# Output projection of a memory attention: eight column tiles of 512 tokens replaced by Strassen's seven products with 256 tokens moving

## The chip, the cores and the metric

The kernel runs on one core of one Trainium2 chip. The metric is the device time of one launch in microseconds (us). Before the change the median of three runs is 795.74 us (794.84 to 796.38). The engines are named as in the profile: PE is TensorE, PEld its weight loads, DVE is VectorE, ACT is ScalarE, POOL is GpSimd and SP is SyncE, which issues most of the transfers.

## The reference, cut to what matters

One decoder layer works on 512 tokens of 1024 features in float32. A mixer is followed by a cross-attention of 4 heads (256 features each) into 256 memory tokens, and by a gated feed-forward layer:

```python
o = jnp.einsum("bhsm,bmhd->bshd", probs, v).reshape(bsz, s, D_MODEL)
return o @ w_o                                   # (512 x 1024) @ (1024 x 1024)
...
h = h + memory_cross_attention(rmsnorm(h, xattn_norm[l]), rmsnorm(mem, mem_norm[l]), w_q[l], w_kv[l], w_o[l])
h = h + swiglu(rmsnorm(h, ffn_norm[l]), w_gate_up[l], w_down[l])
```

The change is in `o @ w_o` and in the addition of its result to `h`.

## The kernel before, in words

**Precision.** A float32 product is made of three float32r matmuls: each operand is split into a rounded part ("hi", a cast on ACT) and the rest ("lo", a subtraction on DVE). `mm3` (L116 to L119) multiplies hi by hi, hi by lo and lo by hi into one PSUM accumulation. A weight unit is 128 x 1024 elements. It is loaded into a `raw` tile, cast to `whi` on ACT (L203), and its rest `wlo` is computed on DVE (L205).

**The order of the work.** `SPEC` is a list of strings, and each string is a slot. A token such as `o:3` or `U:0.1.0` names an item. In step t the kernel emits, in turns, what follows the matmuls of slot t-1 (`post`), what prepares slot t+1 (`prep`) and the loads and splits of the weights that slot t+1 needs (`advance`, L1342); then come the matmuls of slot t (`mm`). The framework orders each engine's instructions from this emission order and from what is ready, and adds the waits. There are six PSUM banks for `ps` tiles, and a double bank `pd`.

**The attention's end before.** `O:h` (`i_pv`, L1005) multiplies the probabilities of head h by its values: two PSUM banks, each 128 features x 512 tokens. Its `post` splits each bank into `t_oh` (ACT, L233) and `t_ol` (DVE, L241). Then `o:0` to `o:7` (`i_o`, L1025) each make 128 output features for all 512 tokens: 8 k-tiles x 3 matmuls, with a 128 x 128 piece of `w_o` stationary and 512 tokens moving. The `post` of `o:m` adds the bank to the residual stream `st["h1", m]` (DVE, L1033; features on the partitions, tokens along the free dimension), and scales the halves of 256 tokens by the gain of the next norm into `t_fa` and `t_fb` (ACT, L1039). After each second m it calls `forms("fg", i, ...)`, which prepares the stationary operands of the next layer. The items `H:r.c` (`i_turn`, L1198) transpose `h1` into token-major tiles.

**Strassen's products, as the next layers have them.** `product` (L1051) computes one of seven products of a 2 x 2 block multiplication in Winograd's form. `forms` (L1159) makes the seven token-side operands of one pair of k-tiles: 4 casts on ACT, and on DVE 4 additions or subtractions of 256 columns, 3 rests of 512 columns and one of 256. `load_strassen` (L148) and `split_unit` (L183) make the seven weight-side operands of a chunk. Quadrants are loaded through SP. Products 5 and 7 add a second quadrant by an accumulating transfer from the POOL queue (L172). Product 6 is an accumulating transfer from one SBUF tile into another (L211). Product 3 is an addition on DVE (L194). The products run in the order 1, 2, 5, 6, 3, 7, 4: 1, 6, 7 and 4 accumulate in bank pair A, 5 and 3 in B, 2 is C. After each product its bank is added to what it belongs to, so a product that continues in a bank waits until the bank was read. In these layers the tokens are stationary (128 x 128) and 512 columns of weights move.

In the item names of `SPEC`, `U:b.f.part` is product f of block b of the gate and up projection, `d` is the down projection, and `V:f` is product f of the values of the memory. Part 0 means the first chunk (pairs 0 and 1 of k-tiles), part 1 the second (pairs 2 and 3), parts 2 and 3 one pair each of the second.

Of the kernel before, what the change touches and what calls it, by code (L numbers as in the profile page):

```python
# [13 lines left out]
P = 128  # L14
# [14 lines left out]


CHUNKS = [("g", b, ks, 512) for b in range(5) for ks in ((0, 1), (2, 3))] + [("g", 5, (0, 1, 2, 3), 256)]
CHUNKS += [("v", 0, (0, 1), 512), ("v", 0, (2, 3), 512)]
CHUNKS += [("d", p, ks, 512) for p, ks in ((0, (0, 1)), (0, (2, 3)), (1, (4, 5)), (1, (6, 7)), (2, (8, 9)), (2, (10,)))]
XBC_ORDER = [8, 10, 0, 1, 2, 3, 9, 11, 4, 5, 6, 7]

# [26 lines left out]
def hybrid_block(ctx: ExitStack, tc: tile.TileContext, a: dict, out: bass.AP,  # L62
# [185 lines left out]
    add_unit("dt", a["w_dt"], KT * 96)  # L248
    idx = 0
    for name, cnt in (("xbc", 12), ("z", 8), ("v", 8), ("pw", 2), ("op", 8), ("os", 8),  # L250
                      ("k", 8), ("q", 8), ("o", 8)):
        for m in range(cnt):
            add_unit((name, m), wu[idx], 1024)
            idx += 1
# [750 lines left out]
    def i_pv(h):  # L1005
        it = Item()

        def mm():
            it.ps = []
            for d in range(2):  # L1010
                ps = PS("o")
                it.ps.append(ps)
                o = (h % 2) * 256 + d * P
                for mt in range(2):
                    vh, vl = st["V", mt, h // 2]
                    xh, xl = st["P", h, mt]
                    mm3(ps, vh[:, o:o + P], vl[:, o:o + P], xh, xl, mt == 0, mt == 1)

        def post():
            yield from splits([("o", 2 * h + d) for d in range(2)], [("o", 512)] * 2, it.ps)  # L1020

        it.mm, it.post = mm, post
        return it

    def i_o(m):  # L1025
        it = Item(keys=[("o", m)])

        def mm():
            proj(hold(it, "wo"), ready[("o", m)], [st["o", k] for k in range(8)])

        def post():
            h = st["h1", m]
            nc.vector.tensor_tensor(out=h, in0=h, in1=it.ps, op=ALU.add)  # L1033
            yield
            i, c = m // 2, m % 2
            if c == 0:
                st["F", i] = T("fa"), T("fb")
            for k in range(2):
                nc.scalar.activation(st["F", i][k][:, 256 * c:256 * c + 256], h[:, 256 * k:256 * k + 256],  # L1039
                                     AF.Identity, scale=col(V_FFN + m))  # L1040
            yield
            if c == 1:
                yield from forms("fg", i, *st["F", i])

        it.mm, it.post = mm, post
        return it


# [2 lines left out]
    def product(stage, block, f, part):  # L1051


        x = {"g": "fg", "d": "ff", "v": "mn"}[stage]
        tts = 1 if stage == "v" else 2
        chunks = [c for c, ch in enumerate(CHUNKS) if ch[0] == stage and ch[1] == block]
        pairs = [(c, i, n) for c in chunks for n, i in enumerate(CHUNKS[c][2])]
        width = CHUNKS[chunks[0]][3]
        begins, ends = part in (None, 0), part in (None, 1, 3)
        if part is not None:  # L1060
            one = chunks[min(part, 1)]
            pairs = [p for p in pairs if p[0] == one]
            if part >= 2:
                pairs = pairs[part - 2:part - 1]
            chunks = [one] if part < 3 else []
        it = Item(keys=[("s", c, f) for c in chunks])

        def mm():
            bank = (stage, BANK[f])
            if f in (1, 2, 5) and begins:  # L1070
                if bank == ("v", "A"):
                    st["vAB"] = psum.tile([P, 1024], F32, tag="pd", name=nm("vAB"), bufs=1)
                    st[bank] = [st["vAB"][:, 0:512]]
                elif bank == ("v", "B"):
                    st[bank] = [st["vAB"][:, 512:1024]]
                else:
                    st[bank] = [PS(stage + BANK[f]) for _ in range(tts)]
            it.ps = [t[:, :width] for t in st[bank]]
            for tt in range(tts):
                ts_ = slice(tt * P, (tt + 1) * P)  # L1080
                first = f in (1, 2, 5) and begins
                for c, i, n in pairs:
                    wh, wl = ready[("s", c, f)]
                    ws = slice(width * n, width * n + width)
                    xh, xl = st["X", x, f, i]
                    for p, w in ((xh, wh), (xl, wh), (xh, wl)):
                        nc.tensor.matmul(it.ps[tt], p[:, ts_], w[:, ws], start=first,  # L1087
                                         stop=(c, i, n) == pairs[-1] and p is xh and w is wl, skip_group_check=True)
                        first = False

        it.mm = mm
        return it, ends, width
# [221 lines left out]
    def num(t):  # L1314
# [8 lines left out]
        "o": i_o, "U": i_gu, "Y": i_turnff, "H": i_turn, "d": i_down, "G": i_gain,  # L1323
    }
    for line in (spec or SPEC):
        its = []
# [87 lines left out]
def _pack(inp):  # L1414
# [25 lines left out]
    u += [mtile(g["w_o"], m) for m in range(8)]  # L1440
    w_u = np.stack([f(t) for t in u])
    wd = g["w_down"].reshape(JF // 2, 2, P, 2, 512)
    wg = g["w_gate_up"].reshape(KT // 2, 2, P, 2, FF)
    wv2 = wkv[:, 1024:].reshape(KT // 2, 2, P, 2, 512)
    w_s = np.zeros((len(CHUNKS), 4, P, 1024), z32)
    for c, (stage, b, pairs, n) in enumerate(CHUNKS):
        for q, (r, k) in enumerate(((0, 0), (0, 1), (1, 0), (1, 1))):
            for j, i in enumerate(pairs):
                src = {"d": lambda: wd[i, k, :, r], "v": lambda: wv2[i, k, :, r],
                       "g": lambda: wg[i, k, :, r, 512 * b:512 * b + n]}[stage]  # L1450
                w_s[c, q, :, n * j:n * j + n] = src()
    dtp = np.zeros((KT, P, 96), z32)
# [43 lines left out]
```

## Time and profile before

| what | value |
|---|---|
| median of three runs | 795.74 us (794.84 to 796.38) |
| the profiled execution: device time, span | 796.13 us, 794.4 us |
| granted TensorE clock | 0.996 |
| PE busy | 782.7 us (99%), 3844 matmuls |
| PEld, DVE, ACT busy | 659.0, 632.9, 496.5 us |
| matmuls of the output projection (`wo`) | 192, starts from 411.2 to 456.0 us |

The span runs from the first to the last instruction of the profiled execution; 1.73 us of its device time lie outside. Stretches such as 411 to 456.4 are microseconds from the start of the span. A duration in the trace is that of one instruction from start to end; neighbouring instructions on an engine overlap, so what an instruction costs in a full queue is read from start to start.

### The profile page before, as it was taken

To read this page: it belongs to the slowest core of one execution; us is meant where nothing else is said; L and a number is where in the kernel's file an instruction comes from. 1 tells how busy PE (TensorE), PEld (TensorE's weight loads), DVE (VectorE), ACT (ScalarE), POOL (GpSimd) and SP (SyncE) were. 2 spreads that over 40 slices of the span, in tenths; PEclk is the share of its full clock that TensorE was granted. 3 is DMA by queue.
4 is the path that set the end of the run, shared out by engine and by line. 5 is a ranking of instruction groups with operands and counts; after the bars stand their busy time and mean duration, and the time that the engine had idled before them with its cause. 6 is when DMAs were issued, how large, how long until landed. Compare 5 with 4: busy or idle time off the path is not lost.

```text
span 794.4 us, 10540 instructions
## 1 busy us (share of the span) xinstructions
PE 782.7 (99%) x3844; PEld 659.0 (83%) x3844; DVE 632.9 (80%) x937; ACT 496.5 (63%) x791; POOL 49.8 (6%) x66
## 2 busy tenths in 40 slices
PE   9999999999999999999999999999999999999995
PEld 7878888888888889888888888888888888888984
DVE  7999969999895799675766667888866788867897
ACT  8668699657953547455655695665455665455845
POOL 0000000000000000000000011011101011101000
PEclk9999999999999999999999999999999999999998
DMA  8253335124475235765355268797779797869602
GB/s 331 90 172 106 114 92 179 54 100 132 153 261 162 97 106 149 170 176 171 132 131 142 72 135 228 176 263 148 247 159 282 179 245 164 248 156 269 163 14 106
DMA packets 41283, 128.62 MB, mean 162 GB/s; under 512 B 4864, under 2 KB 7296, under 8 KB 41232
## 3 DMA queue, kind: packets, MB, share of 16 engines
q1 hardware_dynamic: 33024, 99.30, 36.8%
q0 software_dynamic: 8064, 28.58, 19.8%
q8 instruction: 30, 0.49, 0.2%
q14 instruction: 21, 0.17, 0.1%
q10 hardware_dynamic: 144, 0.07, 0.0%
HBM read 116.63 MB, written 2.13 MB: 149 GB/s over the span
## 4 chain that ended last, share of the span: by engine, by line
PE 86%; DVE 8%; ACT 2%; DMA 1%; issue 1%; SPq 0%; DVEq 0%
PE gA L1087 15%; PE gB L1087 8%; PE dA L1087 5%; PE gC L1087 4%; PE dB L1087 2%; PE vAB L1087 2%; DVE wlo L205 2%; PE wo L117 2%; PE wo L119 2%; PE op L119 2%; PE op L117 2%; PE op L118 2%; PE q L117 2%; PE os L117 2%; PE q L118 2%; PE os L119 2%
## 5 line engine op out<-in xcount | busy, mean ns | idle before, releaser
L203 ACT CAST whi<-raw 128x1024 fp32r<-128x1024 f32 (+1 forms) x125 | 129.0, 1040 | 96.0 <-issue 14.2
L205 DVE TENSOR_TENSOR wlo<-raw,whi 128x1024 fp32r<-128x1024 f32 (+1 forms) x125 | 149.9, 1208 | 32.0 <-ACT whi L203 30.9
L203 ACT CAST whi<-wq 128x1024 fp32r<-128x1024 f32 (+1 forms) x76 | 77.4, 1028 | 76.2 <-PE gA L1087 19.3
L205 DVE TENSOR_TENSOR wlo<-wq,whi 128x1024 fp32r<-128x1024 f32 (+1 forms) x76 | 90.2, 1193 | 39.8 <-ACT whi L203 39.6
L172 POOL DMA_DIRECT2D raw<-w_s x38 | 32.7, 863 | 644.4 <-DVE t_vx L868 311.5
L1087 PE MATMUL gA<-whi,t_xh 128*128 128x512 f32 (+1 forms) x192 | 71.7, 373 | 0.0
L1087 PE MATMUL gA<-wlo,t_xh 128*128 128x512 f32 (+1 forms) x192 | 71.4, 372 | 0.0
L1087 PE MATMUL gA<-whi,t_xl 128*128 128x512 f32 (+1 forms) x192 | 71.3, 371 | 0.0
L1087 PEld LDWEIGHTS gA<-wlo,t_xh 128*128 128x128 f32 x192 | 36.2, 188 | 6.3
L1087 PEld LDWEIGHTS gA<-whi,t_xl 128*128 128x128 f32 x192 | 36.2, 188 | 6.2
L1087 PEld LDWEIGHTS gA<-whi,t_xh 128*128 128x128 f32 x192 | 36.2, 188 | 6.2
L1103 ACT ACTIVATE t_gu<-t_gu,s 128x512 f32<-128x512 f32 (+1 forms) x24 | 16.4, 688 | 31.7 <-DVE t_gu L1099 31.7
L1087 PE MATMUL dA<-whi,t_xh 128*128 128x512 f32 x88 | 34.1, 392 | 0.4 <-DVE t_hT L1244 0.2
L1087 PE MATMUL dA<-whi,t_xl 128*128 128x512 f32 x88 | 34.2, 389 | 0.0
L1087 PE MATMUL dA<-wlo,t_xh 128*128 128x512 f32 x88 | 34.1, 390 | 0.0
L194 DVE TENSOR_TENSOR wq<-wq,wq 128x1024 f32<-128x1024 f32 (+1 forms) x19 | 22.5, 1193 | 13.5 <-DMA wq<-raw 13.4
L1087 PE MATMUL gB<-whi,t_xq 128*128 128x512 f32 (+1 forms) x96 | 27.5, 371 | 0.0
L117 PE MATMUL z<-t_uh,whi 128*128 128x512 f32 x64 | 25.2, 394 | 0.4 <-ACT t_uh L233 0.4
L1165 ACT CAST t_xh<-t_x 128x512 fp32r<-128x512 f32 x30 | 18.6, 621 | 10.5 <-DVE t_x L1184 6.4
L117 PE MATMUL wo<-t_oh,whi 128*128 128x512 f32 x64 | 25.2, 394 | 0.0
L117 PE MATMUL v<-t_uh,whi 128*128 128x512 f32 x64 | 25.1, 392 | 0.0
L117 PE MATMUL q<-t_hgh,whi 128*128 128x512 f32 x64 | 25.1, 392 | 0.0
(401 smaller groups left out, 2242.5 us busy)
## 6 DMA issues: line engine op xcount, KB each, us to landing
raw<-w_u SPq DMA_DIRECT2D x68, 512.0 KB, 3.4
raw<-w_s SPq DMA_DIRECT2D x54, 512.0 KB, 4.4
wq<-w_s SPq DMA_DIRECT2D x36, 512.0 KB, 5.4
raw<-w_s POOLq DMA_DIRECT2D x36, 512.0 KB, 7.3
wq<-raw POOLq DMA_DIRECT2D x17, 512.0 KB, 7.8
t_x<-xT SPq DMA_DIRECT2D x16, 256.0 KB, 5.6
t_abc<-d_acs SPq DMA_DIRECT2D x16, 256.0 KB, 4.4
out<-t_hT SPq DMA_DIRECT2D x8, 256.0 KB, 2.3
```

Source lines behind the costliest of these rows:

```text
L117: nc.tensor.matmul(ps, whi, xhi, start=start, stop=False)
L118: nc.tensor.matmul(ps, whi, xlo, start=False, stop=False)
L119: nc.tensor.matmul(ps, wlo, xhi, start=False, stop=stop)
L172: nc.gpsimd.dma_start(sw[c, f][:, :n], quad("11" if f == 7 else "22"), accum_op=ALU.add)
L194: add = nc.vector.tensor_tensor(out=sw[c, 3][:, :n], in0=sw[c, 3][:, :n], in1=sw[c, 6][:, :n], op=ALU.add)
L203: nc.scalar.copy(hi[:, :n], raw[:, :n])
L205: nc.vector.tensor_tensor(out=lo[:, :n], in0=raw[:, :n], in1=hi.bitcast(F32)[:, :n], op=ALU.subtract)
L1087: nc.tensor.matmul(it.ps[tt], p[:, ts_], w[:, ws], start=first, stop=(c, i, n) == pairs[-1] and p is xh and w is wl, skip_group_check=True)
L1103: st["silu"] = nc.scalar.activation(g, g, AF.Silu, scale=st["r3",][:, c:c + 1])
L1165: nc.scalar.copy(h if w is None else h[:, w], src)
```

## The change

The eight items `o:0` to `o:7` become the seven products of a Strassen multiplication, named `W:f` in the order list. `w_o` moves from the weight units to two chunks of quadrants. The post of `O:h` now copies its two banks into `t_fa` and `t_fb` (ACT) and calls `forms("ao", h, ...)`. A product of this stage runs through the new `turned`: a 128 x 128 piece of the weights is stationary, and a half of 256 tokens moves, so that the result is feature-major as `h1` is. Four feature tiles share two banks. After each product four additions of 256 columns put it into `h1`. The gain scaling and `forms("fg", ...)` for pairs 0 and 1 follow product 3, those for pairs 2 and 3 product 4. The transposes `H:0.0` to `H:0.3` move behind product 4. The first block of the next layer takes its second chunk pair by pair.

```diff
-CHUNKS += [("v", 0, (0, 1), 512), ("v", 0, (2, 3), 512)]
+CHUNKS += [(x, 0, ks, 512) for x in "vo" for ks in ((0, 1), (2, 3))]
...
-    ... "O:3", "o:0", "o:1",
-    "o:2", "o:3", "o:4 H:0.0", "o:5 H:0.1", "o:6 H:0.2", "o:7 H:0.3",
-    "U:0.1.0 H:1.0 H:1.1", "U:0.2.0 H:1.2 H:1.3", "U:0.5.0", "U:0.1.1 U:0.2.1", "U:0.5.1", ...
+    ... "O:3", "W:1.0", "W:2.0", "W:5.0", "W:1.1 W:2.1", "W:5.1", "W:6", "W:3", "W:7", "W:4 H:0.0 H:0.1 H:0.2 H:0.3",
+    "U:0.1.0 H:1.0 H:1.1", "U:0.2.0 H:1.2 H:1.3", "U:0.5.0", "U:0.1.2 U:0.2.2", "U:0.1.3 U:0.2.3", "U:0.5.1", ...
...
@@ in i_pv, the item O:h
         def post():
-            yield from splits([("o", 2 * h + d) for d in range(2)], [("o", 512)] * 2, it.ps)
+            F = T("fa"), T("fb")
+            for k in range(2):
+                for d in range(2):
+                    nc.scalar.copy(F[k][:, 256 * d:256 * d + 256], it.ps[d][:, 256 * k:256 * k + 256])
+            yield
+            yield from forms("ao", h, *F)
...
+    def i_o(f, part=None):
+        it, ends, _ = product("o", 0, f, part)
+        def post():
+            r, k, sign = INTO[f]
+            for t in range(4):
+                h = st["h1", 4 * r + t][:, 256 * k:256 * k + 256]
+                nc.vector.tensor_tensor(out=h, in0=h, in1=it.ps[t // 2][:, 256 * (t % 2):256 * (t % 2) + 256],
+                                        op=ALU.add if sign > 0 else ALU.subtract)
+            yield
+            if f in (3, 4):
+                for i in (2 * r, 2 * r + 1):
+                    F = T("fa"), T("fb")
+                    for q in (1, 0):
+                        for c in range(2):
+                            m = 2 * i + c
+                            nc.scalar.activation(F[q][:, 256 * c:256 * c + 256],
+                                                 st["h1", m][:, 256 * q:256 * q + 256], AF.Identity,
+                                                 scale=col(V_FFN + m))
+                    yield
+                    yield from forms("fg", i, *F)
+        it.post = post if ends else None
+        return it
...
@@ in product, called where the stage is "o"
+        def turned():
+            for t in range(4):
+                o = slice(256 * (t % 2), 256 * (t % 2) + 256)
+                first = f in (1, 2, 5) and begins and t % 2 == 0
+                for c, i, n in pairs:
+                    wh, wl = ready[("s", c, f)]
+                    ws = slice(512 * n + P * t, 512 * n + P * t + P)
+                    xh, xl = st["X", x, f, i]
+                    for p, w in ((xh, wh), (xl, wh), (xh, wl)):
+                        nc.tensor.matmul(it.ps[t // 2][:, o], w[:, ws], p, start=first,
+                                         stop=(c, i, n) == pairs[-1] and p is xh and w is wl, skip_group_check=True)
+                        first = False
```

`INTO` (L1231, which the down projection uses too) says for each product into which half r of the output features and which half k of the tokens it is added, and with which sign: 1 and 2 into (0, 0), 6 and 3 into (0, 1), 5 and 7 into (1, 1), 4 into (1, 0).

More of the change, by code (lines that the diff above doesn't have):

```diff
@@ L250, in hybrid_block @@
     for name, cnt in (("xbc", 12), ("z", 8), ("v", 8), ("pw", 2), ("op", 8), ("os", 8),
-                      ("k", 8), ("q", 8), ("o", 8)):
+                      ("k", 8), ("q", 8)):
         for m in range(cnt):
@@ L1019, in post @@
         def post():
-            yield from splits([("o", 2 * h + d) for d in range(2)], [("o", 512)] * 2, it.ps)
+            F = T("fa"), T("fb")
[4 more added lines that the diff above has]
+            yield from forms("ao", h, *F)
         it.mm, it.post = mm, post
         return it
[L1025 to L1029, printed above, removed]
+    def i_o(f, part=None):
+        it, ends, _ = product("o", 0, f, part)
         def post():
-            h = st["h1", m]
-            nc.vector.tensor_tensor(out=h, in0=h, in1=it.ps, op=ALU.add)
-            yield
[L1035 to L1045, printed above, removed]
+            r, k, sign = INTO[f]
[3 more added lines that the diff above has]
+                                        op=ALU.add if sign > 0 else ALU.subtract)
+            yield
+            if f in (3, 4):
[10 more added lines that the diff above has]
+        it.post = post if ends else None
         return it
@@ L1051, in product @@
     def product(stage, block, f, part):
-        x = {"g": "fg", "d": "ff", "v": "mn"}[stage]
+        x = {"g": "fg", "d": "ff", "v": "mn", "o": "ao"}[stage]
         tts = 1 if stage == "v" else 2
@@ L1078, in mm @@
             it.ps = [t[:, :width] for t in st[bank]]
+            if stage == "o":
+                return turned()
             for tt in range(tts):
@@ L1322, in hybrid_block @@
         "r2": lambda: rm(rms2), "rt": i_r2t, "q": i_q, "S": i_score, "T": i_ptr, "V": i_v2, "vf": i_memforms, "O": i_pv,
-        "o": i_o, "U": i_gu, "Y": i_turnff, "H": i_turn, "d": i_down, "G": i_gain,
+        "W": i_o, "U": i_gu, "Y": i_turnff, "H": i_turn, "d": i_down, "G": i_gain,
     }
@@ L1439, in _pack @@
     u += [mtile(g["w_q"], m) for m in range(8)]
-    u += [mtile(g["w_o"], m) for m in range(8)]
     w_u = np.stack([f(t) for t in u])
@@ L1443, in _pack @@
     wg = g["w_gate_up"].reshape(KT // 2, 2, P, 2, FF)
+    wao = g["w_o"].reshape(KT // 2, 2, P, 2, 512)
     wv2 = wkv[:, 1024:].reshape(KT // 2, 2, P, 2, 512)
@@ L1449, in _pack @@
                 src = {"d": lambda: wd[i, k, :, r], "v": lambda: wv2[i, k, :, r],
+                       "o": lambda: wao[i, k, :, r],
                        "g": lambda: wg[i, k, :, r, 512 * b:512 * b + n]}[stage]
```

4 rows, old and new, of the table SPEC are left out of this document.

## The prediction

> **What bounds the kernel now.** I read the page first (span, busy shares, the chain that ended last), then PE's list of waits (us in total, times, longest), then the stretches of time.
>
> ```profile
> span 794.4 us, 10540 instructions
> PE 782.7 (99%) x3844; PEld 659.0 (83%) x3844; DVE 632.9 (80%) x937; ACT 496.5 (63%) x791; POOL 49.8 (6%) x66
> PE 86%; DVE 8%; ACT 2%; DMA 1%; issue 1%; SPq 0%; DVEq 0%
> ```
>
> ```profile
> PE warm L384 <- DVE ones L100: 1.2, 1, 1.2
> PE s L117 <- ACT whi L130: 0.7, 1, 0.7
> PE yo L119 <- DVE t_prl L241: 0.4, 1, 0.4
> PE z L117 <- ACT t_uh L233: 0.4, 1, 0.4
> PE dA L1087 <- DVE t_hT L1244: 0.2, 1, 0.2
> ```
>
> PE is the bound. Its listed waits are 2.9 us in all, none of them around the projection. So what PE saves there is saved in full, and what it waits in addition is lost in full. The question is which engine has room. Columns of the next rows: the stretch and its length, then busy us (instructions) of PE, PEld, DVE, ACT and POOL, the clock, the DMA share, GB/s.
>
> ```profile
> 400.20:412.80 12.60, 12.60 (x61) 10.48 (x60) 9.88 (x21) 7.81 (x18) 1.70 (x2) 1.00 0.69 160
> 411.00:456.40 45.40, 45.40 (x208) 37.54 (x207) 26.11 (x41) 23.51 (x44) 2.55 (x3) 1.00 0.37 93
> 480.00:500.00 20.00, 20.00 (x90) 16.53 (x90) 14.84 (x16) 9.62 (x12) 3.42 (x4) 1.00 0.91 233
> ```
>
> In the projection (411 to 456.4) DVE is busy for 26.1 of 45.4 us: 19 us of room, all of which the change will claim.
>
> **PE's part.** Start and duration of single matmuls, and of one weight load:
>
> ```profile
> 411.22 0.39 PE L117 MATMUL wo<-t_oh,whi 128*128 128x512 f32 x1
> ...
> 438.20 0.39 PE L119 MATMUL wo<-t_oh,wlo 128*128 128x512 f32 x1
> ```
>
> ```profile
> 397.23 0.28 PE L117 MATMUL sc<-t_kTh,t_qh 128*128 128x256 f32 x1
> ...
> 399.27 0.28 PE L119 MATMUL sc<-t_kTh,t_ql 128*128 128x256 f32 x1
> ```
>
> ```profile
> 397.35 0.19 PEld L119 LDWEIGHTS sc<-t_kTh,t_ql 128*128 128x128 f32 x1
> ```
>
> From 411.22 to 438.20 lie 119 steps of one 512-column matmul (five items of 24 matmuls): 0.2267 us each. In the scores 17 steps of one 256-column matmul, each with a load of its own, take 2.04 us: 0.120. The old stage has 8 x 8 x 3 = 192 matmuls: 43.5 us. The new one has 4 feature tiles x 4 pairs x 3 = 48 per product, 336 in all: 40.3 us. Strassen's 7/8 alone would give 38.1; two matmuls of 256 columns cost 0.240 where one of 512 costs 0.227, which takes 2.2 back. **PE saves 3.2 us.** The transposes of `h1` stay; they only move.
>
> [...]
>
> **DVE's part.** What an instruction costs in a full queue is read from start to start:
>
> ```profile
> 424.30 0.42 DVE L1174 TENSOR_TENSOR t_x<-t_fa,t_fb 128x256 f32<-128x256 f32 x1
> 424.64 0.42 DVE L1175 TENSOR_TENSOR t_x<-t_fb 128x256 f32<-128x256 f32 x1
> ...
> 426.58 1.46 DVE L1169 TENSOR_TENSOR t_xl<-t_x,t_xh 128x512 fp32r<-128x512 f32 x2
> 427.96 0.68 DVE L1033 TENSOR_TENSOR t_x<-t_x,wo 128x512 f32<-128x512 f32 x1
> 428.61 1.23 DVE L205 TENSOR_TENSOR wlo<-raw,whi 128x1024 fp32r<-128x1024 f32 x1
> ...
> 477.03 2.36 DVE L205 TENSOR_TENSOR wlo<-wq,whi 128x1024 fp32r<-128x1024 f32 x2 [1.67 <-ACT whi L203]
> ```
>
> ```profile
> L194 DVE TENSOR_TENSOR wq<-wq,wq 128x1024 f32<-128x1024 f32 x18 | 21.8, 1222 | 13.5 <-DMA wq<-raw 13.4
> ```
>
> ```profile
> L241 DVE TENSOR_TENSOR t_ol<-o,t_oh 128x512 fp32r<-128x512 f32 x8 | 5.4, 690 | 2.5 <-ACT t_oh L233 2.4
> ```
>
> One `forms` is 3.66 us (424.30 to 427.96). A weight rest is 1.14 (two last 2.36, one 1.22), and so is product 3's addition, of the same length. A 256-column addition is 0.34, a 512-column one from PSUM 0.65. The new additions are 256 columns from PSUM, which no row shows: between 0.34 and 0.65; I take 0.34, half of 0.65 being 0.33.
>
> Removed: 8 rests `t_ol` (5.4) and 8 additions into `h1` (5.2). Added: four `forms("ao")` (14.6), 14 weight rests for 8 (6.8), two additions for product 3 (2.3), 28 additions of 256 columns (9.5). Net 33.2 - 10.6 = **22.6 us more DVE work**, against 19 us of room.
>
> When is it wanted? I take the time from 400.2 (the scores of head 3 are done) to the start of `W:3`, before which nearly all of it is due. PE wants `W:3` after `O:3` and 192 matmuls: 411.2 + 192 x 0.120 = 434.2. By then DVE must have done:
>
> - what is left of the attention, with the first weight rest: 9.88 - 5.4 = 4.5 (the stretch 400.20:412.80 without `t_ol`);
> - four forms: 14.6;
> - nine further weight rests (products 1, 2, 5, 6, 3; two chunks each): 10.3;
> - two additions for product 3: 2.3;
> - the additions after products 1, 2 and 5, 12 x 0.34: 4.1.
>
> That is 35.8 us of work in 34.0 us. How densely DVE can run, where each form goes back and forth between ACT and DVE, is bounded by its densest stretch (160:180), its densest among the products (760:780) and the next one there (660:680):
>
> ```profile
> 160.00:180.00 20.00, 19.59 (x92) 16.09 (x91) 19.90 (x34) 11.32 (x18) 0.00 (x0) 1.00 0.36 118
> 660.00:680.00 20.00, 19.86 (x92) 16.18 (x92) 18.50 (x31) 10.95 (x16) 1.71 (x2) 1.00 0.67 154
> 760.00:780.00 20.00, 20.00 (x90) 16.34 (x89) 19.27 (x32) 12.21 (x23) 0.00 (x0) 1.00 0.08 14
> ```
>
> At 19.90 of 20 the work takes 36.0 us and is 2.0 late; two things can come off: 1.4 (the additions after product 2, whose bank nobody takes until the transposes) and 0.7 (the second chunk is first wanted 6 matmuls in). So the lower bound is no wait. At 18.50 it takes 38.7 and is 4.7 late. The nearest row, 19.27, gives 37.2 us, 3.2 late; I take off the 0.7, which is certain, and leave the additions where they are emitted, ahead of the later weights. **PE waits 2.5 us, bounds 0 and 4.7**; this wait is made of several, and comes once.
>
> Where it is seen first follows from the queue:
>
> ```profile
> 404.93 1.44 DVE L241 TENSOR_TENSOR t_ol<-o,t_oh 128x512 fp32r<-128x512 f32 x2
> 406.29 1.28 DVE L241 TENSOR_TENSOR t_Pl<-pT,t_Ph 128x512 fp32r<-128x512 f32 x2
> ```
>
> The rests `t_Pl` of head 3 stand behind the posts of `O:0` and `O:1`. What they emit grows from 2.9 us of `t_ol` to two forms (7.3). `O:3` wants its first `t_Pl` at about 408.7; if both forms run first, it is there at 404.9 + 7.3 + 0.6 = 412.8, 4.1 late, and if only head 0's does, at 409.2. PE has nothing else to run: `W:1.0` needs the banks that `t_Pl` still reads. Behind the waiting `O:3` stand its copies, head 3's forms, and for those `W:1.1`. It is the same DVE work seen earlier, so I don't add it.
>
> **ACT, transfers and banks** I cost at nothing.
>
> ```profile
> L203 ACT CAST whi<-raw 128x1024 fp32r<-128x1024 f32 x122 | 127.5, 1050 | 96.0 <-issue 14.2 <-PE wo L118 11.8 <-PE op L118 10.8
> L1165 ACT CAST t_xh<-t_x 128x512 fp32r<-128x512 f32 x30 | 18.6, 621 | 10.5 <-DVE t_x L1184 6.4 <-DVE t_x L1175 4.0
> L1165 ACT CAST t_xq<-t_fb 128x256 fp32r<-128x256 f32 x15 | 6.0, 402 | 0.0
> wq<-raw POOLq DMA_DIRECT2D x17, 512.0 KB, 7.8
> ```
>
> ACT in the same 34 us: at most 7.8 of the attention's end, 10 casts of weights (10.5), 16 copies at the 256-column price (6.4), four forms of 3 x 0.62 + 0.40 (9.0): 33.7 with the `t_oh` casts still in it, some 29 without them. It is not first; were DVE faster, ACT would be next. The transfers grow from eight units of 0.5 MB to 14 from HBM and two between SBUF tiles: 8 MB in 40 us or 200 GB/s, and the next layer runs at 233 GB/s and a share of 0.91 without a wait of PE (480:500). The last one due is product 6's accumulation for the second chunk: issued after the second `W:2` split, a slot ahead of `W:2.1`, with 7.8 to landing, 1.05 and 1.22 for the split, 10.1 us in all; PE's work from there is `W:1.1`, `W:2.1`, `W:5.1` and 6 matmuls, 9.4. It is 0.7 late if no other wait comes first, and hidden behind the 2.5. Banks: a product that follows in the same bank (7, then 4) waits for additions, but the loop over feature tiles is the outer one, so the first bank is free for half a product, 2.9 us, before it is wanted.
>
> **The seam into the next layer** I also cost at nothing.
>
> ```profile
> 456.40 0.69 DVE L1033 TENSOR_TENSOR t_x<-t_x,wo 128x512 f32<-128x512 f32 x1 [3.29 <-PE wo L119]
> 459.67 0.69 DVE L1178 TENSOR_TENSOR t_xl<-t_fa,t_xh 128x512 fp32r<-128x512 f32 x1
> ```
>
> From the last addition to the end of the first rest of the last form it took 4.0 us (456.40 to 460.36). Now two pairs follow product 4: 4.0 + 3.7 = 7.7 us. PE has cover: transposes and the slots `U:0.1.0`, `U:0.2.0`, `U:0.5.0`, 36 x 0.227 = 8.2 us without the transposes. Pairs 0 and 1 have the time of `W:7` and `W:4`, 11.5 us, for 13.4 of DVE work (two forms 7.3, eight additions 2.7, three weight rests 3.4), of which 1.5 (the last form's later rests) can follow. If the cover fails, it costs up to 1.9.
>
> **Sum.** -3.2 + 2.5 = -0.7. The profiled execution took 796.13, so 795.4; it lies 0.39 above the median, so 795.0 against 795.74.
>
> **Rivals.** A measurement of this kernel can tell about 0.2% (1.6 us) from no change.
>
> *DVE keeps up.* The weight rests move into DVE's gaps before 400 and the additions after product 2 later; the wait is 0.5: 795.74 - 2.7 = 793.0. For it: 19.90 of 20 in 160:180. Against it: PE had other work there, here every product waits for forms.
>
> *DVE falls behind further.* The mechanism is the to and fro within each form (ACT idles 10.5 us behind `t_x`, the row of L1165). It decides from a density of 0.906 down: there the wait is 4.8 and the sum +1.6. At 0.89 DVE takes 40.2 us, ends at 440.4, 5.5 late after the 0.7: +2.3, 798.0. For it: the ring `O:3`, copies, forms, `W:1.1` leaves DVE with little choice. Against it: 18.50 and 19.27 where the products were fed the same way.
>
> *Weight loads bound the smaller matmuls.* At one load of 0.188 per matmul 336 take 63.2 us, not 40.3: +19.7, 815. The rows of the scores speak against it: loads of 0.19 start every 0.12. [...]
>
> **How the numbers follow.** Forecast 0.42, DVE keeps up 0.32, falls behind 0.24, loads 0.02. So faster 0.32, same 0.42, slower 0.26. The forecast's own range is 794.1 to 797.3 (the wait's bound 4.7). For 8 in 10 I go down to the full saving, 792.4, and up to 798.4, where the density is about 0.88.
>
> **What would show it.** PE: 336 matmuls in the stage, 0.120 apart where they run. DVE over nine tenths busy from 400 to 436. PE waits naming `t_Pl` before `O:3`, `t_xl` before `W:1.1`, or `wlo` before `W:6` and `W:3`, 2.5 us in all, and none at `U:0`. I am wrong in the term if the step isn't 0.120, in the bound if the waits name DMA or ACT, in the place if they are at `U:0`.

## The result and the profile after

The changed kernel took 810.37 us (median of 4 runs, 809.87 to 811.82), the kernel before beside it 795.66 (794.84 to 796.38): a ratio of 1.0187, 95% interval 1.0175 to 1.0199. It is slower by 14.7 us. I had forecast 795.0 and a range up to 798.4: the prediction was wrong. In a later session one launch of the kernel before and the profiled one of the spread kernel ran at a mean granted clock of 0.56 and took 1320 and 1311 us; the ratios leave them out, and that trace is not used.

The profiled execution of the changed kernel took 809.87 us, 13.7 more than that of before. From its page the span, the busy shares and the chain that ended last:

```profile
span 808.0 us, 10957 instructions
PE 785.5 (97%) x3988; PEld 665.7 (82%) x3988; DVE 655.4 (81%) x989; ACT 510.3 (63%) x821; POOL 55.1 (7%) x72
PE 81%; DVE 10%; ACT 5%; issue 2%; DMA 1%; DVEq 0%; ACTq 0%
```

The chain that was 86% PE now runs through DVE and ACT for 15% (10% before). PE's list of waits from 396 to 500 us (us in total, times, longest), where before had none:

```profile
PE o L116 <- ACT t_Ph L232: 3.7, 1, 3.7
PE gA L1095 <- ACT t_xh L1187: 3.1, 2, 2.1
PE hT L1227 <- ACT t_hT L1231: 2.5, 2, 2.0
PE oA L1109 <- ACT t_fb L1022: 0.6, 1, 0.6
PE gB L1095 <- ACT t_hT L1231: 0.6, 1, 0.6
PE gC L1095 <- ACT t_hT L1231: 0.4, 1, 0.4
PE gA L1095 <- DVE t_xl L1200: 0.3, 1, 0.3
```

All but one name ACT, and they lie in two places: at `O:3` (seam 1, into the projection) and at the transposes and `U:0` (seam 2, out of it). The stretches (columns as in the prediction: length, busy us of PE, PEld, DVE, ACT, POOL, then the granted clock, the DMA share and GB/s) show something more:

```profile
400.00:411.00 11.00, 7.40 (x37) 5.84 (x35) 10.51 (x26) 8.18 (x24) 1.74 (x2) 1.00 0.54 102
411.00:420.00 9.00, 8.29 (x32) 6.89 (x33) 6.92 (x16) 5.64 (x16) 0.00 (x0) 0.62 0.00 0
420.00:440.00 20.00, 20.00 (x169) 20.00 (x168) 15.39 (x26) 7.33 (x8) 0.86 (x1) 1.00 0.51 156
458.00:470.00 12.00, 9.47 (x51) 7.43 (x51) 9.30 (x16) 11.51 (x24) 1.71 (x2) 0.99 0.66 140
470.00:480.00 10.00, 7.04 (x23) 4.56 (x21) 8.39 (x18) 7.10 (x13) 0.86 (x1) 0.84 0.61 138
```

Behind each seam's waits the clock is below 1 (0.62 from 411 to 420, 0.84 from 470 to 480). On PE's own rows at seam 1 (start, duration, matmul, idle before):

```profile
411.13 0.73 PE L116 MATMUL o<-t_Ph,t_Vh 128*128 128x512 f32 x2 [3.73 <-ACT t_Ph L232]
412.44 0.58 PE L1109 MATMUL oA<-t_xh,whi 128*128 128x256 f32 x1 [0.57 <-ACT t_fb L1022]
...
413.46 0.63 PE L118 MATMUL o<-t_Ph,t_Vl 128*128 128x512 f32 x1
413.89 0.63 PE L116 MATMUL o<-t_Ph,t_Vh 128*128 128x512 f32 x1
...
418.58 0.28 PE L1109 MATMUL oA<-t_xh,wlo 128*128 128x256 f32 x1
418.70 0.29 PE L1109 MATMUL oA<-t_xh,whi 128*128 128x256 f32 x1
...
420.50 0.28 PE L1109 MATMUL oC<-t_xh,whi 128*128 128x256 f32 x1
...
458.43 0.29 PE L1109 MATMUL oA<-t_xh,wlo 128*128 128x256 f32 x1
```

After the wait, matmuls of 512 columns stand 0.43 apart instead of 0.227, at a granted clock of 0.50 (412.4 to 418.4), until 418.4, 7 us behind the wait. Then the projection runs without a wait: from 420.50 (`W:2.0`) to 458.43 lie 311 steps, 37.93 us with five transposes of 0.11 put among them, so 0.120 a step.

I divide the layer's middle by four marks, the same in every kernel with the products: the start of `O:0`, the first matmul into `oC` (`W:2.0`), the last into `oA` (`W:4`), and the first of `U:0.3`.

| kernel after, us | measured | without waits, from before's steps | lost |
|---|---|---|---|
| `O:0` to first `oC` | 22.38 | 14.7 (11.83 in before up to the projection, + 24 x 0.120) | 7.7 |
| first `oC` to last `W` | 37.93 | 37.9 | 0 |
| last `W` to `U:0.3` | 35.28 | 25.4 (24.52 in before, + 7 x 0.12 for 27 transposes instead of 20) | 9.9 |

At seam 1 waits of 4.30 (3.73 + 0.57) leave 3.4 of the 7.7 to the half clock; at seam 2 waits of 6.9 leave 3.0 of the 9.9 to the clock and smaller gaps. 7.7 + 9.9 less the 3.2 saved is 14.4; the three stretches measure 95.59 us against 81.11, 14.5 more. (`O:0` itself started 1.3 earlier; the span is 13.6 longer.)

What stands ahead of the late casts is read from ACT's queue. At seam 1:

```profile
406.50 0.64 ACT L1022 COPY t_fa<-o 128x256 f32<-128x256 f32 x2
...
409.97 0.62 ACT L1187 CAST t_xh<-t_x 128x512 fp32r<-128x512 f32 x1 [0.94 <-DVE t_x L1206]
410.50 1.07 ACT L232 CAST t_Ph<-pT 128x512 fp32r<-128x512 f32 x2
```

The transposes of head 3's weights (`T:3`) were done at 405, but the casts `t_Ph` stand behind the forms of head 0 and the copies and forms of head 1, and these in turn wait for DVE. At seam 2:

```profile
460.41 0.58 ACT L1231 COPY t_hT<-hT 128x512 f32<-128x512 f32 x1
461.02 0.64 ACT L1234 ACTIVATE t_sq<-t_hT 128x512 f32<-128x512 f32 x1
...
465.52 0.64 ACT L1234 ACTIVATE t_sq<-t_hT 128x512 f32<-128x512 f32 x1
466.06 0.18 ACT L1234 ACTIVATION_READ_ACCUMULATOR t_sq<-t_hT 128x1 f32 x1
466.15 0.89 ACT L1045 ACTIVATE t_fb<-t_x,vec 128x256 f32<-128x256 f32 x2
```

Four copies and squares of the transposed residual (`H:0.0` to `H:0.3`), 460.41 to 466.15, stand ahead of the scaling for pair 2. DVE had made this pair's last two additions some 6 us before (the first two of these three, 0.34 each):

```profile
458.96 1.07 DVE L1036 TENSOR_TENSOR t_x<-t_x,oA 128x256 f32<-128x256 f32 x3
...
461.16 0.41 DVE L1036 TENSOR_TENSOR t_x<-t_x,oA 128x256 f32<-128x256 f32 x1
```

PE waits for pair 2's cast until 469.35:

```profile
469.35 0.89 PE L1095 MATMUL gA<-whi,t_xh 128*128 128x512 f32 x2 [2.15 <-ACT t_xh L1187]
...
480.24 0.66 PE L1227 MATMUL hT<-ident,t_x 128*128 128x128 f32 x4 [1.95 <-ACT t_hT L1231]
```

The second row is what comes of it later: the copies of `H:1.0` and `H:1.1` stand behind pair 3's forms and hold the banks that the last transposes want.

### The profile page after: what moved, and what is told of

It is laid out like the page before. It is cut to its first block, busy times and chain, and to the rows that moved or that the text cites. A ratio compares the mean times of both kernels' runs of the same rounds, so it can differ in the third digit from the quotient of the medians.

```text
span 808.0 us, 10957 instructions
## 1 busy us (share of the span) xinstructions
PE 785.5 (97%) x3988; PEld 665.7 (82%) x3988; DVE 655.4 (81%) x989; ACT 510.3 (63%) x821; POOL 55.1 (7%) x72
## 3 DMA queue, kind: packets, MB, share of 16 engines
q0 software_dynamic: 8928, 31.72, 21.9%
## 4 chain that ended last, share of the span: by engine, by line
PE 81%; DVE 10%; ACT 5%; issue 2%; DMA 1%; DVEq 0%; ACTq 0%
PE gA L1095 14%; PE gB L1095 7%; PE dA L1095 5%; PE gC L1095 3%; DVE wlo L204 3%; PE dB L1095 2%; PE vAB L1095 2%; PE op L118 2%; PE op L116 2%; PE op L117 2%; PE q L116 2%; PE os L116 2%; PE q L117 2%; PE os L118 2%; PE q L118 2%; PE os L117 2%
## 5 line engine op out<-in xcount | busy, mean ns | idle before, releaser
L202 ACT CAST whi<-raw 128x1024 fp32r<-128x1024 f32 (+1 forms) x123 | 126.8, 1039 | 87.5 <-PE op L117 14.1
L204 DVE TENSOR_TENSOR wlo<-raw,whi 128x1024 fp32r<-128x1024 f32 (+1 forms) x123 | 147.3, 1208 | 33.6 <-ACT whi L202 32.6
L202 ACT CAST whi<-wq 128x1024 fp32r<-128x1024 f32 (+1 forms) x84 | 85.9, 1030 | 80.7 <-PE dA L1095 17.8
L204 DVE TENSOR_TENSOR wlo<-wq,whi 128x1024 fp32r<-128x1024 f32 (+1 forms) x84 | 100.0, 1196 | 41.2 <-ACT whi L202 40.9
L171 POOL DMA_DIRECT2D raw<-w_s x42 | 36.2, 868 | 636.9 <-DVE t_vx L867 310.3
L193 DVE TENSOR_TENSOR wq<-wq,wq 128x1024 f32<-128x1024 f32 (+1 forms) x21 | 24.9, 1196 | 15.6 <-DMA wq<-raw 15.6
L1187 ACT CAST t_xh<-t_x 128x512 fp32r<-128x512 f32 x38 | 23.6, 622 | 12.4 <-DVE t_x L1206 6.5
L1191 DVE TENSOR_TENSOR t_xl<-t_x,t_xh 128x512 fp32r<-128x512 f32 x38 | 25.2, 686 | 0.4
```

What stands on the lines that cost most here:

```text
L171: nc.gpsimd.dma_start(sw[c, f][:, :n], quad("11" if f == 7 else "22"), accum_op=ALU.add)
L193: add = nc.vector.tensor_tensor(out=sw[c, 3][:, :n], in0=sw[c, 3][:, :n], in1=sw[c, 6][:, :n], op=ALU.add)
L202: nc.scalar.copy(hi[:, :n], raw[:, :n])
L204: nc.vector.tensor_tensor(out=lo[:, :n], in0=raw[:, :n], in1=hi.bitcast(F32)[:, :n], op=ALU.subtract)
L1187: nc.scalar.copy(h if w is None else h[:, w], src)
L1191: nc.vector.tensor_tensor(out=dst, in0=src, in1=h.bitcast(F32), op=ALU.subtract)
```

## The experiments

My theory after this reading: the projection itself does what was forecast; the loss is the order of ACT's queue at two seams, and the clock behind each wait. The rivals: the waits only move when the order is changed, because the sum of ACT's or DVE's work is too large; or the smaller matmuls cost time that no wait shows.

**Seam 1 alone.** Head 1's forms become an item of their own behind `T:3`:

```diff
+            if h == 1:
+                st["F", h] = F
+            else:
+                yield from forms("ao", h, *F)
...
-    "V:4 S:3 O:0", "O:1", "T:3 O:2", "O:3"
+    "V:4 S:3 O:0", "O:1", "T:3 f:1 O:2", "O:3"
```

> The changed kernel, with head 1's forms emitted after the split of head 3's probabilities (t_Ph, t_Pl) in place of ahead of it. Theory A (queue order): the 3.7 us for which O:3 waits on t_Ph, and the 5.4 us at half clock behind it, come from two heads' forms standing ahead of that split on ACT and DVE; with one of them moved the wait is 1 us or less, the clock stays at 1.0 in the ten us that follow, and the time falls by 6 to 7.5 us, to 803 to 804.5. Theory B (my ledger: DVE has more work than time until W:3, in whatever order): the wait moves to W:1.0, W:1.1 or W:3 and at most 2 us are gained, 808.4 or more.

Measured: 807.01 us, ratio 1.0136 (1.0119 to 1.0153), 3.4 us less than the changed kernel. PE's waits at this seam:

```profile
PE oA L1115 <- ACT t_fb L1022: 1.4, 1, 1.4
PE o L116 <- ACT t_Ph L232: 0.8, 1, 0.8
```

They fell from 4.3 to 2.2 us (0.8 of them for `t_Ph`), the clock from 411 to 420 is 1.00, and `O:0` to `oC` takes 17.51 instead of 22.38. Of the 4.9 us gained here, 1.6 was lost at seam 2 (36.89 for 35.28). So theory A holds for the wait and the clock; the time lies between the two theories' ranges. (The profiled launch itself took 809.49: it began `O:0` 2.4 us later than the changed kernel's, 1.7 of them from a wait at 55 us, which this edit does not touch.)

**The clock at seam 1.** Sixteen matmuls whose result nothing reads fill the wait ahead of `O:3`:

```diff
+            if h == 3:
+                for _ in range(16):
+                    nc.tensor.matmul(fill[:, 0:512], vh[:, 0:P], vh, start=True, stop=True)
```

> The changed kernel, with 16 matmuls of 512 columns between O:2 and O:3 whose result nobody reads (3.6 us of PE work, just the length of the wait). No data comes earlier. If the half clock after the wait follows from PE having been idle, the matmuls after O:3 starts are 0.227 us apart in place of 0.43, and some 2.9 us are gained: 807 to 808. If they are slow because of what else runs then (ACT and DVE at the same operands), nothing is gained: 810.

Measured: 810.63 us, 1.0177 (1.0157 to 1.0197), no gain. In place it did what was expected: clock 1.00 from 411 to 420, and `O:0` to `oC` 19.59, 2.8 less. But seam 2 took 37.68, 2.4 more, with waits of 6.2 us in all (6.9 in the changed kernel) and a lower clock (0.76 and 0.83 from 470 to 490, for 0.84 and 1.00):

```profile
411.00:420.00 9.00, 8.32 (x54) 7.01 (x53) 8.35 (x18) 7.76 (x19) 0.00 (x0) 1.00 0.00 0
470.00:480.00 10.00, 7.47 (x24) 5.03 (x22) 7.51 (x13) 7.79 (x15) 0.86 (x1) 0.76 0.52 118
480.00:490.00 10.00, 9.30 (x35) 7.38 (x36) 4.66 (x11) 8.04 (x18) 0.00 (x0) 0.83 0.17 54
```

So how much clock a seam loses is not fixed by its waits alone. It differs from launch to launch too: of this kernel's four, one took 807.92 us at a mean clock of 0.995, and two took 811.2 at 0.990 and 0.991. A gain at one seam can only be trusted once the other is free of waits.

**Seam 2: transposes earlier on PE.**

```diff
-    "W:7", "W:4 H:0.0 H:0.1 H:0.2 H:0.3",
+    "W:7 H:0.0 H:0.1 H:0.2 H:0.3", "W:4",
```

> The changed kernel, with the transposes H:0.0 to H:0.3 in the slot of W:7 in place of that of W:4, so that their copies and squares on ACT (four of about 1.2 us) are done before product 4 ends. Theory A (ACT's queue at the second seam): the scaling for pairs 2 and 3 starts at once after the additions, some 4.8 us earlier; PE's waits at the start of the next layer (6.9 us) fall to 2 or less; 803 to 805.5. Theory B (DVE has fallen behind there): the waits stay, less than 1.5 us gained.

Measured: 812.38 us, 1.0206 (1.019 to 1.0221), 2.0 us above the changed kernel, with intervals that just overlap; the waits at seam 2 stayed (7.1 us). On ACT nothing was won: the copies and squares kept their place ahead of the scaling,

```profile
461.20 0.58 ACT L1231 COPY t_hT<-hT 128x512 f32<-128x512 f32 x1
...
466.94 0.89 ACT L1045 ACTIVATE t_fb<-t_x,vec 128x256 f32<-128x256 f32 x2
```

and PE lost the transposes as cover behind `W:4`. What matters is the place in ACT's queue, not when PE is done with the transposes.

**Both of these.** Seam 1's forms late and the transposes early:

> Both order changes (head 1's forms after the split of head 3's probabilities; transposes with product 7). If the two seams are independent and are the whole loss, the gains add: 796 to 798, still short of the 792.5 that PE's matmuls alone would give, with what is left in small waits. If DVE's ledger is the limit, a wait of 2 to 4 us on t_xl or wlo appears inside the W products, which the late start hid until now: 799 to 802.

Measured: 810.09 us, 1.0172 (1.0149 to 1.0194), above both ranges: the gains did not add, and no wait for `t_xl` or `wlo` stands inside the `W` products. Seam 1 kept most of its gain (19.04 to `oC`, with a clock of 0.81 from 411 to 420), seam 2 took 37.83 with a clock of 0.68 from 470 to 480.

**Seam 2: transposes later.** Two transposed blocks share the double bank, and the first is emitted behind `U:0.2.0`, so that ACT scales and forms pairs 2 and 3 first:

```diff
-    "W:7", "W:4 H:0.0 H:0.1 H:0.2 H:0.3",
-    "U:0.1.0 H:1.0 H:1.1", "U:0.2.0 H:1.2 H:1.3", "U:0.5.0", "U:0.1.2 U:0.2.2", "U:0.1.3 U:0.2.3", "U:0.5.1",
+    "W:7", "W:4", "U:0.1.0", "U:0.2.0 H:0.0", "U:0.5.0 H:0.1", "U:0.1.2 U:0.2.2 H:1.0", "U:0.1.3 U:0.2.3 H:1.1", "U:0.5.1",
```

> The changed kernel with the eight transposes into the next layer (`H:`) done two at a time in the double bank, and the first of them only behind `U:0.2.0`, so that on ScalarE the copies and squares of the transposed residual stand behind the scaling and the forms of pairs 2 and 3 instead of ahead of them. Theory A (the second half of the loss is ScalarE's queue: four copies and squares, some 4.9 us, ahead of the scaling that waits only for `W:4`): the first wait of the stage for a cast of pair 2 goes from 2.15 us to under 0.5, the waits behind `W:4` from 6.9 us to under 2, the half clock there goes too, and the stretch from the last `W` matmul to `U:0.3` falls from 35.3 us to 26 to 29; time 801 to 804. Rival B (ScalarE simply has too much work there, and the order only decides who is late): the waits move to the copies (the double bank, or the gate's `r3`) and come to some 6 us again; time 808 to 811. Rival C (the loss given back elsewhere, as with the earlier filler): in this stretch the gain shows, the total does not move.

Measured: 804.56 us, 1.0107 (1.0092 to 1.0122), 5.8 us less than the changed kernel. Seam 2:

```profile
PE hT L1228 <- ACT t_hT L1235: 2.9, 3, 1.2
PE gA L1094 <- ACT t_gu L1130: 0.6, 1, 0.6
PE gB L1094 <- DVE t_xl L1190: 0.2, 1, 0.2
```

The casts of pair 2 are in time. Of 6.9 us of waits 3.7 are left, now mostly at the double bank (2.9), whose copies stand close together on ACT; last `W` to `U:0.3` is 29.96, and the clock there is 1.00. Theory A holds for the casts, but its sizes don't: waits of 3.7 for under 2, 29.96 for 26 to 29, and a time 0.6 above its range. Rival B has a part in it, the waits for the bank.

**Both seams, and `T:3` earlier.** The last kernel with head 1's forms late as well, and then with one more line:

> The kernel of the late transposes with the forms of head 1 behind the post of `T:3` as well: both seams mended, the products themselves as in the changed kernel. Theory A (the whole loss of 14.7 us lies in the two seams, waits and the half clock behind them, and the products save 3 us): O:0 to the first `oC` 17.5 us, last `W` to `U:0.3` 26 to 29, time 796 to 800, that is within 0.5 per cent of the kernel before. Rival D (the matmuls with 256 columns, or the additional work of VectorE, cost time that is not seen as a wait in the two seams): time 803 or more with both seams free of waits.

Measured: 802.30 us, 1.0076 (1.0061 to 1.0091); `O:0` to `oC` 18.93, last `W` to `U:0.3` 29.97. Neither theory's time: both seams still wait (2.2 and 3.7 us). Seam 1 has the same two waits as with its repair alone (0.8 and 1.4), where it took 17.51 at a clock of 1.00; here the clock from 411 to 420 is 0.84, and with the transposes early it was 0.81.

```diff
-    "V:4 S:3 O:0", "O:1", "T:3 f:1 O:2", "O:3",
+    "S:3 V:4 O:0", "T:3 O:1", "f:1 O:2", "O:3",
```

> As the kernel with both seams mended, and the transposes of head 3's weights (`T:3`) one place earlier, ahead of `O:1`, with `S:3` ahead of `V:4`, so that the casts of these weights stand ahead of the copies of heads 1 and 2 on ScalarE. If what is left at the first seam (0.8 us for a cast of `t_Ph`, 1.4 us for a copy that frees a bank) comes from that order: no wait named t_Ph before `O:3`, O:0 to the first `oC` 15 to 16.5 us (the new place of `T:3` adds its 1.1 us to this stretch), 1 to 2 us less than with both seams mended. If it comes from the sum of ScalarE's work: the wait moves to the banks of `W:1.0`, and the time is the same within 0.5 us.

Measured: 801.81 us, 1.0076 (1.006 to 1.0093). No wait names `t_Ph`, as expected, and `O:0` to `oC` fell to 16.91, just above the range, since PE now waited 1.1 for `t_p`. The time fell by only 0.5, but not for the reason that the second outcome gives, a wait at the banks of `W:1.0`: what was won here was lost at seam 2. Seam 2, where nothing was changed and the waits were 2.9 for the bank as before, took 31.72 instead of 29.97, with the clock at 0.73 (470 to 480) for 1.00. Its rows:

```profile
472.18 1.09 PE L1234 MATMUL hT<-ident,t_x 128*128 128x128 f32 x8 [0.60 <-ACT t_hT L1241]
474.44 1.79 PE L1234 MATMUL hT<-ident,t_x 128*128 128x128 f32 x8 [1.16 <-ACT t_hT L1241]
477.39 1.97 PE L1234 MATMUL hT<-ident,t_x 128*128 128x128 f32 x8 [1.16 <-ACT t_hT L1241]
...
479.68 0.63 PE L1100 MATMUL gA<-whi,t_xl 128*128 128x512 f32 x1
480.11 0.63 PE L1100 MATMUL gA<-wlo,t_xh 128*128 128x512 f32 x1
```

The second eight transposes already take 1.79 us where the first took 1.09, so the clock had fallen after waits of 0.60 and 1.16.

**Moving the transposes in the kernel before.** One part of the change alone, with no Strassen product in the projection:

```diff
-    "o:4 H:0.0", "o:5 H:0.1", "o:6 H:0.2", "o:7 H:0.3",
+    "o:4", "o:5", "o:6", "o:7 H:0.0 H:0.1 H:0.2 H:0.3",
```

> The kernel before, its projection unchanged, with nothing but the four transposes `H:0.0` to `H:0.3` moved from behind `o:4` to `o:7` to behind `o:7`, all four, as the changed kernel has them behind `W:4`. On ScalarE four copies and squares then stand in the midst of the scaling of the last pair. Theory A (the place of the transposes makes a part of the loss by itself): the casts of pair 3 come 3.5 to 5 us later, TensorE waits before `U:0.1.1` or `U:0.2.1` 1 to 4 us, with a clock below 1 behind it; time 797 to 801. Rival E (only with all scaling behind the last product is there a loss; here pairs 0 to 2 are done early and cover it): no wait over 0.5 us between `o:7` and `U:0.3`, time 795 to 796.5.

Measured: 800.07 us, 1.005 (1.0035 to 1.0065), 3.8 us slower than before. Theory A's time is right; its place is not. No cast of pair 3 kept PE waiting, but the bank of a later transpose and a bank of `U:0` did, and the clock fell to 0.83 from 470 to 480:

```profile
470.36 0.66 PE L1205 MATMUL hT<-ident,t_x 128*128 128x128 f32 x4 [1.61 <-ACT t_hT L1209]
471.59 0.79 PE L1087 MATMUL gB<-whi,t_xh 128*128 128x512 f32 x1 [0.57 <-ACT t_hT L1209]
```

So moving the transposes, which changes no arithmetic, and that I had costed at nothing ("they only move"), costs 3.8 us by itself in the kernel before.

**Spreading the transposes.** On top of the kernel with `T:3` earlier, the four pairs are spread, the copies of the second half go to DVE, and the first silus wait for the squares in an item of their own (`R`):

```diff
-                nc.scalar.copy(st["h", c, r], ...)
+                (nc.vector.tensor_copy if r else nc.scalar.copy)(st["h", c, r], ...)
...
-    "U:0.2.0 H:0.0", "U:0.5.0 H:0.1", "U:0.1.2 U:0.2.2 H:1.0", "U:0.1.3 U:0.2.3 H:1.1", "U:0.5.1", "U:0.6", "U:0.3",
+    "U:0.2.0", "U:0.5.0", "U:0.1.2 U:0.2.2", "U:0.1.3 U:0.2.3 H:0.0", "U:0.5.1", "U:0.6.0 H:0.1", "U:0.6.1 H:1.0", "U:0.3 H:1.1 R",
```

> On top of the kernel with both seams mended and `T:3` early: the four pairs of transposes are spread between `U:0.1.3`, the two halves of `U:0.6`, and `U:0.3`, with 2.7 us or more of matmuls between two of them; the copies of the second half of the tokens go from ScalarE to VectorE, which idled 4.7 us there; and the first two silus of block 0 wait for the squares in an item of their own. Theory A (what was left at the second seam, 2.9 us of waits for the double bank and some 3 us of half clock behind them, comes from the copies standing close together on ScalarE): no wait of hT over 0.3 us, clock 1.00 from 458 to 490, last `W` to `U:0.3` 27 to 28.5 us instead of 31.7 (with one pair more behind `U:0.3`), time 795 to 797, at most 1.5 us above what the sum of TensorE's work gives (792.5 plus the 2.2 us lost at the first seam). Rival B (ScalarE has too much work there whatever the order): the bank copies of `U:0.1` and `U:0.5` become late instead, 3 us or more of waits named t_gu, time 799 to 802.

Measured: 795.93 us, 1.0003 (0.9994 to 1.0012), 5.9 less than without it, in theory A's range; its signs at seam 2 are read in the trace of the next kernel, which has the same seam 2. Then with `T:3` behind `O:1` (`"S:3 V:4 O:0", "O:1 T:3", "f:1 O:2", "O:3"`):

> As the spread kernel, but `T:3` behind `O:1` instead of ahead of it, since ahead of it TensorE waited 1.1 us for the normalised weights of head 3. If the wait for t_p is only a matter of 2.7 us more cover: it goes, the casts of `t_Ph` come at about the same time (behind the copies of `O:1`), and O:0 to the first `oC` is 15 to 16.3 us against 16.9; time 0.5 to 1.5 us below the spread kernel, 794 to 796. If the wait moves to `O:3` (t_Ph or t_Pl late by the copies of `O:1`): the same time within 0.5 us.

Measured: 796.11 us, 1.0008 (0.9999 to 1.0017), no difference. The second outcome: the wait for `t_p` is gone, but one of 1.3 for `t_Ph` took its place, and `O:0` to `oC` is 16.91, as in the kernel with `T:3` ahead of `O:1`. Seam 2 in its trace has no wait in PE's list at all, the clock is 1.00, and last `W` to `U:0.3` takes 25.32 (with one pair of transposes behind it), less than the 27 to 28.5 expected:

```profile
470.00:480.00 10.00, 9.76 (x50) 7.91 (x51) 6.60 (x9) 9.63 (x21) 0.23 (x1) 1.00 0.80 211
```

ACT is still busy for 9.63 of 10 us here, so a full ACT need not hold PE up. But not only the order changed: with four copies on DVE, ACT is busy for 30.56 of the 37 us from 453 to 490, where the kernel with `T:3` earlier had 33.17 and the changed kernel 32.25. No run parts the order from these 2.6 us.

**Head 0's forms late too** (`if h < 2`, `"f:0 f:1 O:2"`):

> As the spread kernel with `T:3` behind `O:1`, and the forms of head 0, like those of head 1, only behind the casts of `t_Ph` and subtractions of `t_Pl` that `O:3` waits for (both heads' forms in turn, step by step). In that kernel TensorE still waited 1.3 us for `t_Ph`, since ScalarE made head 0's forms first. If only the order matters: no wait before `O:3` over 0.3 us, `W:1.0` starts without one, since it needs just the first cast and the first rest of heads 0 and 1; O:0 to the first `oC` 14.9 to 15.7 us against 16.9; time 793.8 to 795.0, that is 0.8 to 2 us below the kernel before, what is left of the 3.2 us that the products save. If ScalarE and VectorE together have too much work between `O:0` and `W:2.0`: the wait goes to `W:1.0` or `W:5.0` (t_xh, t_xl), 1 to 2 us, time 795.3 to 796.5, no difference from before.

Measured: 795.52 us against 795.91, 0.9995 (0.9986 to 1.0004): no difference that can be told. `O:0` to `oC` took 15.04 as expected; the wait went to `W:5.0` instead, 0.6 us of the 1 to 2 that the other outcome named, and for a copy that frees a bank (`t_fb`), not for `t_xh` or `t_xl`:

```profile
PE oB L1114 <- ACT t_fb L1021: 0.6, 1, 0.6
PE gB L1100 <- DVE t_xl L1208: 0.2, 1, 0.2
```

Its span is 793.4, 1.0 below that of before. PE stands idle there for 1.2 us between 400 and 480 (from the stretches), so 2.0 of the 3.2 should be left. Some 1 us I can't place, or 1.6 by the medians: this launch was 0.4 below its kernel's median, and the profiled one of before 0.4 above.

**What a wait costs.** The kernel before with a wait made on purpose: twelve copies on ACT ahead of head 3's casts, their result not read.

```diff
+            if h == 3:
+                for _ in range(12):
+                    nc.scalar.copy(T("sq"), it.ps[1])
```

> The kernel before with one artificial wait and nothing else: behind `T:3`, twelve copies of the transposed weights from PSUM to a scratch tile (about 0.53 us each, 6.4 us; the result is not read) stand on ScalarE ahead of the casts of head 3's `t_Ph`, so that TensorE waits before `O:3` some 4 us. Theory A (the clock falls after a wait of this length and costs as much again in part): the granted clock is 0.6 or so in the 5 to 7 us behind the wait, the projection's first matmuls stand 0.45 apart, and the time rises by the wait and 2 to 4 us more: 801.5 to 804. Rival F (the low clock behind the wait belongs to the new kernel's matmuls, not to the wait): clock 1.00 behind it, the time rises by the wait alone, 799 to 800.5.

Measured: 802.25 us, 1.0078 (1.0065 to 1.0091), 6.3 us more for a wait of 3.8:

```profile
411.38 1.22 PE L117 MATMUL o<-t_Ph,t_Vh 128*128 128x512 f32 x2 [3.79 <-ACT t_Ph L233]
...
413.25 0.63 PE L117 MATMUL o<-t_Ph,t_Vh 128*128 128x512 f32 x1
413.68 0.63 PE L118 MATMUL o<-t_Pl,t_Vh 128*128 128x512 f32 x1
...
416.66 0.63 PE L117 MATMUL wo<-t_oh,whi 128*128 128x512 f32 x1
```

From 411.38 to 417.1 the matmuls stand 0.43 apart: 13 of them, some 0.21 too long each, 2.8 us; 3.8 + 2.8 = 6.6. The clock from 411 to 420 is 0.65, where the kernel before has 1.00. So here the low clock came with the wait, without the new kernel's matmuls.

## Why the prediction was wrong

*PE's part* was right: 0.120 a step, 3.2 us less. No load bound a matmul (loads of 0.19, PEld at 20.00 of 20 from 420 to 440, and the step stayed at 0.120), so the rival of 815 is out.

*DVE's part* was right in its sum and wrong in its consequence. DVE's busy time grew by 22.5 us (632.9 to 655.4); I had 22.6. The additions I could not see in the trace took 0.35 from start to start (four in 1.48):

```profile
434.37 1.48 DVE L1036 TENSOR_TENSOR t_x<-t_x,oB 128x256 f32<-128x256 f32 x4
```

But no product waited for a weight rest or a form. In the changed kernel the hold-up at seam 1 had given DVE time, so that is no proof; in the last kernel, with this hold-up gone, DVE is busy for 32.96 of 36 us (400 to 436, 92%) and PE waits for it nowhere in the projection (0.2 us at `U:0`), not 2.5. That is the lower bound of my range for the term, and the rival *DVE keeps up* in a part of its mechanism: of the ten weight rests that I put between 400 and `W:3`, only seven stand there in that trace (the first from 399.77), so three were done before; the additions after product 2 stayed where they were emitted. DVE over nine tenths busy from 400 to 436 held there, not in the changed kernel (30.84 of 36).

*Seam 1* I had found: `O:3`, held by work of heads 0 and 1, "412.8, 4.1 late". The first matmul of `O:3` came at 411.13, 3.73 late. Two things failed. I wrote "it is the same DVE work seen earlier, so I don't add it"; in truth the wait from DVE's sum never came and this one did, so the 4.3 us stood in place of 2.5. And I put it at the rests `t_Pl`; it was the casts `t_Ph` on ACT, which stood behind the same forms there. ACT "at nothing" was a sum (29 of 34 us); ACT was in fact less busy than that (19.90 from 400.2 to 434.2) and late all the same, because its queue ran in the emitted order and passed on DVE's delays (2.7 us of idle behind `t_x` from 402.7 to 410.5). The two waits and the half clock behind them cost 7.7 us.

*Seam 2* is the step that failed outright: "the seam into the next layer I also cost at nothing". I worked out DVE's 4.0 + 3.7 = 7.7 us against 8.2 of cover, and left out what the moved transposes issue: four copies and squares on ACT, 5.7 us with a weight cast among them (460.41 to 466.15), between the last addition and the scaling. With them the sum is 13.4 against 8.2, 5.2 late, where I had named 1.9 for a failed cover. It is here that 9.9 us went: of the 15.4 between my -0.7 and the measured 14.7, seam 2 makes 9.9 and seam 1 5.2 (7.7 for 2.5). With the transposes behind the scaling the casts of pair 2 were in time, which shows the cause; the kernel before with only the transposes moved loses 3.8 without any product, though by late banks and not by a late cast.

*The clock* was missing from the sum altogether: with smaller gaps it is some 6.4 of the 17.6 us lost at the two seams. I priced a wait at its length; the wait made on purpose costs 1.7 times that. Half clock (0.43 between matmuls of 512 columns for 0.227) lasted 5.7 us behind that wait of 3.79, and 7 behind the one of 3.73 at seam 1, with 0.57 idle in it. In the kernel with `T:3` earlier the clock fell too, to 0.73 from 470 to 480, where no wait was longer than 1.16 us: behind one of 0.60 and one of 1.16 with only eight transposes between. And equal waits met different clocks (0.73 and 1.00 at seam 2; 1.00, 0.84 and 0.81 at seam 1). What sets the clock behind a wait is not shown by any run here.

I had named waits on ACT (against the bound) and waits at `U:0` (against the place) as signs of being wrong. Both came: all but 0.3 of 11.2 us name ACT, and 6.9 stood at seam 2, among the transposes and `U:0`. Transfers cost nothing, as forecast: no wait names a DMA.

What is settled: with the seven products as they are, the order around them changed, the transposes in the double bank and four copies moved to DVE, the whole loss of 14.7 us is gone, so the products themselves did not cause it. What is not: how much of the last 5.9 us is the order and how much the moved copies. And the change gains nothing that can be measured in the best order I found, 0.4 us of the 3.2, interval from 1.1 faster to 0.3 slower.

## What to carry to other kernels

When an item moves, write down what its post issues on each engine's queue, and walk that queue in order past the move; a sum of busy time over the stretch says nothing about who stands behind whom. Where PE is at 99%, price a wait like these (3.7 to 3.8 us) at well over its length (6.3 us for 3.8 here), since the matmuls behind these ran at half clock (0.43 apart for 0.227), and don't judge a repair at one seam while another still waits. The saving of 3.2 us on PE was smaller than the cost of one misplaced group of four copies and squares (3.8 us in the kernel before).

## What I had not expected of the hardware

The granted clock fell to half for 5.7 to 7 us behind the waits of 3.79 and 3.73 (0.50 from 412.4 to 418.4 in the changed kernel): 0.43 between matmuls of 512 columns for 0.227, 0.213 for 0.120 at 256. It fell in one trace also after two short waits (0.60 and 1.16 us, with eight transposes between; 0.73 from 470 to 480), where two other kernels with the same waits kept 1.00. A gain at one seam was lost at another: with the low clock at seam 1 removed (clock 1.00, 2.8 us won there), seam 2 ran at 0.76 and 0.83 and took 2.4 more, and the total stood still; why it fell there is not shown. And weight loads of 0.19 us hid behind matmuls of 0.120 over 336 of them.
